# A two-layer convolutional decoder trunk on one core: other down blocks, no staging in the mixer, 34 weight units not staged

## The chip, the cores and the metric

The kernel runs on one core of one Trainium2 chip. The metric is device time in microseconds (us), the median of several runs, and lower is better. The engines are called as in the profile: PE (matmuls), DVE (vector), ACT (activations), POOL (GpSimd) and SP (here it only issues DMAs).

## What is computed

Two layers work on 1024 prompt tokens and on 8 sequences of 8 sample tokens, T = 1088 columns in all, with a width of 1024. Layer 0's token mixer is a gated short convolution, layer 1's a Conformer convolution module. All is float32.

```python
def short_conv_mixer(x, past, w_in, w_conv, w_out):
    bch = x @ w_in
    b, c, h = jnp.split(bch, 3, axis=-1)
    y, new_past = causal_dwconv(c * h, past, w_conv)
    return (b * y) @ w_out, new_past
def swiglu_ffn(x, w_gu, w_down):
    g, u = jnp.split(x @ w_gu, 2, axis=-1)
    return (jax.nn.silu(g) * u) @ w_down
...
        h = h + mix
        h = h + swiglu_ffn(rms_norm(h, g_ffn[i]), ffn_w_gu[i], ffn_w_down[i])
        gate = jax.nn.sigmoid(rms_norm(h, g_ple[i]) @ ple_w_gate[i])
        h = h + gate * (p[i] @ ple_w_proj[i])
```

The feed-forward has 2816 hidden features, 22 tiles of 128.

## The kernel before

**Products and weights.** Features lie on the 128 partitions and tokens along the columns, so `h` is eight tiles `h0` to `h7` of 128x1088. A float32 product is made of three products of a reduced type (fp32r): each operand is split into a high part (an ACT copy) and a low part (operand less its high part), and high·high, low·high and high·low are summed in PSUM. A weight *unit* is eight blocks of 128x128 (tile `wraw`, 128x1024). `prep_to` (lines 218 to 244) makes its high half on ACT (`whi`) and its low half (`wlo`) in one of two ways: by a POOL subtraction, or, where the unit has been *staged*, by a DMA from `dlo`.

**Staging.** `stage` (line 246) works ahead on the units of later parts, of which several are used more than once. One step handles half a unit: ACT's queue fetches `sraw`, ACT makes `shi`, POOL subtracts, and at the next step ACT's queue stores the result as `dlo`. The store waits for POOL, and whatever ACT has in its queue behind it waits too. A step is issued when a model clock of PE in the builder passes `stage_at`, every `STAGE_EVERY` us. `to_stage` (line 165) is the list of the halves.

**Mixer of layer 0.** `mixer_a` (line 525) calls `hidden` (line 649): `up(f)` computes one of eight activation tiles `act` (three items of eight blocks with the elementwise work on ACT, DVE and POOL), and a down block of n tiles adds, for each of eight outputs j, the sum over its n activation tiles to `h[j]`. `MIX_SPLIT` lists the block sizes. An item is one PSUM tile, of which there are two; `add_h` (line 517) is a DVE addition that frees it.

**End of the mixer.** In the last down block `mixer_end` (line 575) is called after each item. It adds, stores `h` for later, sums the squares for the next norm (`norm_stat`, tiles `sq` and `sqacc`), and makes the operands of the feed-forward (`op_first`, `op_sums`, `op_part`): high and low halves of B11, B21, B22 and of four sums T1 to T4 for each of four k, 28 operands of 128x544 twice. Where each lies is the table `cells`, filled in `last_down` (line 1215): memory of the mixer that has become free. `T4` and `B11` of the last k lend theirs to `sq` first.

**Feed-forward of layer 0, first half.** `ffn0_up` (line 669) computes gate and up of one hidden tile f by seven products in place of eight, each of 24 matmuls of 272 columns, on sums of operands and of weights (Strassen's scheme). The weight sums S1 to S4 (`ws`) of the next f are four DVE subtractions and additions in `pair_sums` (line 301); `pair_cell` (line 312) splits each of the seven weights A11 to S4 into a cell (`w`), those named A by POOL, those named S by DVE. The two raw tiles of a pair are fetched by `pair_fetch` when the cell A22 of the pair before is made. `next_weights(n)` (line 696) says behind which of the seven products which of these steps are issued: `m == 0` issues the sums, and 1 to 4 the cells. Engines carry out their instructions in the order in which they are issued.

**Second half.** `ffn0_down` (line 763) reads the stored hidden tiles back (`act_load`, tile `ta`), splits them (`act_split`: ACT `act`, DVE `act<-ta,act`) and multiplies in down blocks listed in `DOWN_0`, like the mixer's. `early` (line 1271) does this for the first block while the last hidden tile is computed, and loads `h` again in the order `DOWN_J`.

**Layer 1** prepares each unit some two ahead in the same `prep_to`; its feed-forward is run for the two halves of the tokens, so its units are fetched twice, and the last gate's units three times.

Line 129 is the helper through which every operation is issued, so all rows of the profile name it and are told apart by their tiles.

Of the kernel before, what the change touches and what calls it, by code (L numbers as in the profile page):

```python
# [145 lines left out]
class Net:  # L146
# [3 lines left out]
    def __init__(self, ctx, tc, xT, wall, pT, sa, sb, vecs, yT, sa_p, sa_s, sb_p, sb_s):  # L150
        self.ctx, self.tc, self.nc = ctx, tc, Engines(tc.nc)
        self.xT, self.wall, self.pT, self.sa, self.sb, self.vecs = xT, wall, pT, sa, sb, vecs
        self.yT, self.sa_p, self.sa_s, self.sb_p, self.sb_s = yT, sa_p, sa_s, sb_p, sb_s
        first = list(range(N_UNITS_0))
        middle = list(range(N_UNITS_0, N_UNITS_0 + N_PLE + N_PW1))
        proj = list(range(middle[-1] + 1, N_UNITS - N_UNITS_1))
        rest = list(range(N_UNITS - N_UNITS_1, N_UNITS))
        pw1 = middle[-N_PW1:]
        self.order = first + middle + middle[:-N_PW1] + proj[:1] + pw1 + proj[1:] + 2 * rest + rest[-KD:]
        self.raw, self.hi, self.lo = {}, {}, {}  # L160
        self.n_raw = self.n_prep = self.blk = 0
        self.limit = N_MIX
        self.n_conv = 0
        self.pairs, self.cell = {}, {}
        self.to_stage = deque((u, i) for u in dict.fromkeys(self.order[len(first):]) for i in range(2))
        self.staged, self.staging, self.stage_raw = {}, None, deque()
        self.stage_slots, self.stage_at, self.stage_ends = None, 0.0, False
        self.bg = deque()
        self.spare = []
        self.slots = deque(["w"] * self.RING)  # L170
        self.shift_late = True
        self.sums_split = True
        self.lanes = [deque(), deque()]
        self.lane_cost = [0.0, HALF_TILE]
        self.pe_later = []
# [349 lines left out]
    def mixer_a(self, y):  # L525
        nc = self.nc
        g = GJ
        r = self.rg(g)
        self.r2 = self.pu0.tile([P, T], F32, name="r2", bufs=1)
        acts = {}  # L530

        def up(f):
            u = self.pu0.tile([P, UA0_COLS], F32, name="u0", tag="u0")
            nc.gpsimd.memset(u[:, 0:LA], 0.0)
            nc.sync.dma_start(u[:, SMP_A:], self.sa[f])
            usm = smp(u[:, SMP_A:])
            t = self.tmp(g)
            if f == 0:
                psc, psh = self.pair(g, y)
                nc.scalar.activation(t, psc, AF.Copy)  # L540
            else:
                nc.scalar.activation(t, self.item(g, y), AF.Copy)
                self.stage_ends = f == KD - 1
                psh = self.item(g, y)
            nc.vector.tensor_tensor(u[:, LA:LA + SEQ], psh[:, :SEQ], t[:, :SEQ], ALU.mult)
            nc.vector.tensor_tensor(usm[:, :, LA:], smp(psh[:, SEQ:]), smp(t[:, SEQ:]), ALU.mult)
            if f == 0:
                psb = self.item(g, y, self.rms(g, 1, 4))
                b = self.tmp(g)
                nc.scalar.activation(b, psb, AF.Copy)  # L550
                psb = b
                nc.vector.tensor_tensor(self.r2, r, r, ALU.mult)
            for o, i in ((u[:, LA:LA + SEQ], self.r2[:, :SEQ]), (usm[:, :, LA:], smp(self.r2[:, SEQ:]))):
                nc.gpsimd.tensor_tensor(o, o, i, ALU.mult)
            nc.sync.dma_start(self.sa_p[f], u[:, SEQ:SEQ + LA])
            nc.sync.dma_start(smp(self.sa_s[f]), usm[:, :, LS:])
            w = self.vec("a_conv", f, CA)
            q = self.tmp(g)
            for k in reversed(range(CA)):
                for o, i in ((q[:, :SEQ], u[:, k:k + SEQ]), (smp(q[:, SEQ:]), usm[:, :, k:k + LS])):  # L560
# [12 lines left out]
        self.hidden(g, MIX_SPLIT, up, acts, js=MIX_J, last=self.mixer_end)

    def mixer_end(self, i, ps):
# [9 lines left out]
        self.hd[j] = self.pd.tile([P, T], F32, name=f"hd{j}")  # L585
        self.nc.sync.dma_start(self.hd[j], self.h[j])
        k = j - KH
        pool, tag = self.cells["B11", KH - 1] if i % 2 == 0 and i else self.cells["T4", KH - 2]
        stat = lambda: self.norm_stat(g, j, sq=i and pool.tile([P, T], F32, name="sq", tag=tag, bufs=1))
        if i == KD - 1:  # L590
            self.op_first(k)
            self.at_end[3](0)
# [76 lines left out]
    def ffn0_up(self, early):  # L669
# [11 lines left out]
        for f in range(KF):  # L681
# [14 lines left out]
            def next_weights(m):  # L696

                i = f + 1
                if i == KF:
                    return  # L700
                m -= 2 if f < 2 else 1
                if m == 0:
                    self.pair_sums(i)
                for n in {1: self.ORDER[:3], 2: self.ORDER[3:5], 3: self.ORDER[5:6], 4: self.ORDER[6:]}.get(m, ()):
                    self.pair_cell(i, n)
                if m == 4 and i + 1 < KF:
                    self.pair_fetch(i + 1)
# [39 lines left out]
            self.ad[f] = self.pd.tile([P, T], F32, name=f"ad{f}")  # L747
            nc.sync.dma_start(self.ad[f], t)

    def act_load(self, queue):  # L750
        f = len(self.acts)
        low, high = (pool.tile([P, T], F32R, name="act", tag=tag, bufs=1) for pool, tag in self.places.popleft())
        t = self.tmp(GJ, "ta")
        queue.dma_start(t, self.ad[f])
        self.acts.append((high, low))
        return t
# [6 lines left out]
    def ffn0_down(self, swap):  # L763
# [3 lines left out]
        for b, n in enumerate(DOWN_0):  # L767
            last = b == len(DOWN_0) - 1
            loads = []
            for i in range(KD):  # L770
# [3 lines left out]
                if b == len(DOWN_0) - 2 and j == KD - 3:  # L774
                    self.stage_ends = True
                self.add_h(g, j, self.item(g, self.acts[at:at + n]))
                if loads:
                    self.act_split(*loads.pop(0))
                if not last:
                    continue  # L780
# [373 lines left out]
    def run(self):  # L1154
# [35 lines left out]
        self.pps = pool("ps_j", c_ps, space=PSUM, bufs=2)  # L1190
        self.pY = pool("y_j", c_y, side="right", bufs=KD)
        self.pt = pool("t_j", c_t, bufs=4)
        self.pX = pool("x_j", c_x, bufs=4)
        self.pu0 = pool("u0", c_u, bufs=2)
        self.hd, self.ad, self.right, self.sums = {}, {}, {}, {}
        p = pool("stage_m", c_st)
        self.stage_with(self.stage_tiles(p, 0, 2), self.stage_tiles(p, 2, 6))
        self.stage_at = self.STAGE_FROM

        warm = self.pps.tile([P, 512], F32, name="st", tag="m0", bufs=1)[:, :P]  # L1200
        for _ in range(self.WARM):
# [11 lines left out]
            self.norm_stat(GJ, j, nc.vector)  # L1213

        def last_down():
            self.stage_with()
            c_st.close()
            c_u.close()
            c_y.close()
            py = pool("y_16", c_y, side="right")  # L1220
            py2 = pool("y_6", c_y2, side="right")
            self.cells = {}
            free = [(py, f"y{i}") for i in range(2 * KD)]
            for k in range(KH - 1):
                for n in ("B11", "T1"):
                    self.cells[n, k] = py2, f"z{len(self.cells)}"
            for k in range(KH - 1):
                for n in ("B21", "T2", "B22", "T3", "T4"):
                    self.cells[n, k] = free.pop(0)
            self.cells["B11", KH - 1] = free.pop(0)  # L1230
            for n, j in ("B21", 0), ("T1", 4), ("T2", 1), ("B22", 5), ("T3", 2), ("T4", 6):
                self.cells[n, KH - 1] = ph, f"h{j}"

        def before_last():
# [4 lines left out]
        def last_item():  # L1239
            c_x.close()  # L1240
            self.pws = pool("w2", c_x)
            self.ring = deque([(self.pw, f"w{i}") for i in (2, 5, 3, 6)] + [
                (self.pws, f"c{i}") for i in range(4)] + [(self.pw, f"w{i}") for i in (4, 7)])

# [17 lines left out]
        p = pool("stage_u", c_st)  # L1262
        self.stage_with(self.stage_tiles(p, 0, 1), self.stage_tiles(p, 1, 5))
        self.stage_at += self.STAGE_LATE
        py, py2 = self.cells["T2", 0][0], self.cells["B11", 0][0]
        places = [[(py2, f"z{2 * i}"), (py2, f"z{2 * i + 1}")] for i in range(3)]
        places += [[(py, f"y{2 * i}"), (py, f"y{2 * i + 1}")] for i in range(5)]
        self.places = deque(places[i % len(places)] for i in range(KF - DOWN_0[-1]))
        self.acts = []
# [1 line left out]
        def early():  # L1271
# [3 lines left out]
            self.limit = len(self.order)  # L1275
            self.n_conv += 2
            self.fetch_to(self.n_raw + self.RAW)
            t = [self.act_load(nc.sync) for _ in range(DOWN_0[0])]
            self.prep_to(self.n_raw - self.RAW + 1)
            for f in range(DOWN_0[0]):  # L1280
                self.act_split(f, t[f])
# [16 lines left out]
            lambda name, dtype, i=i: py.tile([P, T], dtype, name=name, tag=f"y{i}", bufs=1)[:, :WH]  # L1298
            for i in range(10, 16)]
        self.stage_with(at[:2], at[2:])  # L1300
        c_ya = ExitStack()

        def swap():
# [111 lines left out]
    RMS_AT = {GJ: (0, 2), GA: (3, 6), GB: (1, 4)}  # L1415
    T_BUFS = 5
    COST_B = 1.6
    STAGE_EVERY = 3.75
    STAGE_LATE = 25.0
    STAGE_FROM = 30.0  # L1420
    LAG = 3
    WARM = 12
    RB_GATE = 4
# [123 lines left out]
```

## Time and profile before

| | |
|---|---|
| time, median of 3 runs | 2551.46 us (2551.21 to 2556.66) |
| the profiled execution's own time | 2553.06 us |
| its span in the profile | 2551.3 us |
| mean granted clock of PE | 0.988 of full speed |
| PE busy | 2480.1 us, 97% |
| DVE busy | 1412.5 us, 55% |
| ACT busy | 1000.6 us, 39% |
| POOL busy | 969.9 us, 38% |
| moved by DMA | 462.71 MB, 181 GB/s |

The profile is of one execution; its own time lies 1.76 us above its span (launch and end) and 1.60 above the median of the runs. An engine's busy time is the sum of its instructions. In a row of a timeline stand the start, the duration, the engine, the line, the operation, the tile written and the tiles read, how many like it follow one another (x6) and, in brackets, the idle time of that engine just before and what ended it. In a row of windows, PEclk is the mean clock that PE was granted: 1.00 is 2.4 GHz, and the lower of its two levels is 1.2 GHz.

### The profile page before, as it was taken

How to read it: one execution, taken by the hardware profiler on the slowest of the kernel's cores; microseconds unless marked ns; L12 is line 12 of the kernel's file. 1: busy time of each engine (PE TensorE's matmuls, PEld its weight loads, DVE VectorE, ACT ScalarE, POOL GpSimd, SP SyncE). 2: the span in 40 equal slices, each digit the busy share in tenths (PEclk: the TensorE clock that was granted, in tenths of full speed). 3: DMA queues.
4: the chain of work that ended last, by engine and by line, in shares of the span. 5: the costliest groups of instructions: out<-in, count | busy, mean ns of one | idle time of the engine just before them, and what ended most of it. 6: DMA issues, size and time to landing. Idle time of an engine off the chain costs nothing.

```text
span 2551.3 us, 39084 instructions
## 1 busy us (share of the span) xinstructions
PE 2480.1 (97%) x15590; PEld 2286.9 (90%) x15590; DVE 1412.5 (55%) x1940; ACT 1000.6 (39%) x1377; POOL 969.9 (38%) x662
## 2 busy tenths in 40 slices
PE   9989998899999989999999999999999999999997
PEld 8888997899999989998789897888887999999997
DVE  6122128788888853324587676777874622222235
ACT  5322235344443433325555436444435532222235
POOL 3656554356665645533244233333341210000012
PEclk9999999999999999999999999999999999999999
DMA  4555542366665677643565566555556565555445
GB/s 145 166 166 164 162 129 87 111 204 207 207 210 199 214 266 235 223 149 109 177 211 180 172 176 190 190 183 190 189 175 206 202 246 200 162 164 164 165 165 194
DMA packets 183575, 462.71 MB, mean 181 GB/s; under 512 B 38368, under 2 KB 41824, under 8 KB 183392
## 3 DMA queue, kind: packets, MB, share of 16 engines
q1 hardware_dynamic: 116000, 331.46, 39.5%
q10 hardware_dynamic: 67392, 128.74, 15.9%
q8 instruction: 123, 2.02, 0.3%
q14 instruction: 60, 0.49, 0.1%
HBM read 375.65 MB, written 84.48 MB: 180 GB/s over the span
## 4 chain that ended last, share of the span: by engine, by line
PE 60%; DVE 3%; DMA 2%; ACT 1%; issue 1%; POOL 1%; ACTq 0%; DVEq 0%; POOLq 0%; SPq 0%
PE ps L129 60%; DMA ta<-ad 1%; DVE t L129 1%; POOL sraw L129 1%; DVE ws L129 0%; DMA wlo<-dlo 0%; DVE h L129 0%; DVE acc L129 0%; ACT ua L129 0%; DVE hna L129 0%; DVE nt L129 0%; ACT shi L129 0%; ACT cact L129 0%; DMA wraw<-wall 0%; ACT act L129 0%
## 5 line engine op out<-in xcount | busy, mean ns | idle before, releaser
L129 PE MATMUL ps<-hn,whi 128*128 128x288 f32 (+3 forms) x4416 | 916.5, 324 | 5.7 <-ACT t L129 3.4
L129 PEld LDWEIGHTS ps<-hn,whi 128*128 128x128 f32 x4416 | 693.9, 189 | 61.2 <-ACT t L129 3.7
L129 PE MATMUL ps<-hn,wlo 128*128 128x288 f32 (+3 forms) x2208 | 563.3, 323 | 3.0 <-DMA wlo<-dlo 3.0
L129 PE MATMUL ps<-act,whi 128*128 128x288 f32 (+1 forms) x2496 | 520.1, 333 | 23.6 <-DVE h L129 19.5
L129 PE MATMUL ps<-y,w 128*128 128x272 f32 x3696 | 475.0, 291 | 18.1 <-ACT t L129 6.2
L129 PEld LDWEIGHTS ps<-y,w 128*128 128x128 f32 x3696 | 472.9, 191 | 20.0 <-ACT t L129 6.5
L129 PEld LDWEIGHTS ps<-act,whi 128*128 128x128 f32 x2496 | 393.4, 191 | 64.8 <-DVE h L129 19.1
L129 POOL TENSOR_TENSOR sraw<-sraw,shi 128x512 fp32r<-128x512 f32 x220 | 320.1, 1455 | 203.8 <-ACT shi L129 90.4
L129 PEld LDWEIGHTS ps<-hn,wlo 128*128 128x128 f32 x2208 | 365.5, 189 | 29.9 <-DMA wlo<-dlo 3.2
L129 ACT ACTIVATE whi<-wraw 128x1024 fp32r<-128x1024 f32 (+1 forms) x282 | 293.4, 1042 | 186.7 <-PE ps L129 144.7
L129 DVE TENSOR_TENSOR h<-ps,h 128x1088 f32<-128x1088 f32 (+2 forms) x200 | 184.9, 927 | 245.6 <-PE ps L129 245.3
L129 PE MATMUL ps<-act,wlo 128*128 128x288 f32 (+1 forms) x1248 | 306.0, 331 | 0.0
L129 POOL TENSOR_TENSOR t<-t,r 128x512 f32<-128x512 f32 (+2 forms) x52 | 80.4, 1547 | 538.1 <-ACT t L129 493.0
L129 ACT ACTIVATE shi<-sraw 128x512 fp32r<-128x512 f32 x220 | 138.0, 627 | 359.8 <-POOL sraw L129 355.9
L129 POOL TENSOR_TENSOR sqacc<-sqacc,sq 128x512 f32<-128x512 f32 (+4 forms) x76 | 115.7, 1522 | 314.4 <-ACT sq L129 314.1
L129 DVE TENSOR_TENSOR t<-ps,t 128x544 f32<-128x544 f32 (+3 forms) x155 | 113.6, 743 | 217.6 <-PE ps L129 170.7
L129 PEld LDWEIGHTS ps<-act,wlo 128*128 128x128 f32 x1248 | 201.2, 191 | 18.8
L129 ACT ACTIVATE t<-t 128x512 f32<-128x512 f32 (+4 forms) x106 | 76.0, 718 | 302.1 <-DVE t L129 302.0
L129 POOL TENSOR_TENSOR prod<-prod 128x512 f32<-128x512 f32 x96 | 124.3, 1304 | 182.5 <-ACT prod L129 182.3
L129 POOL TENSOR_TENSOR wlo<-wraw,whi 128x1024 fp32r<-128x1024 f32 (+1 forms) x54 | 134.8, 2499 | 145.3 <-ACT whi L129 141.8
L129 DVE TENSOR_TENSOR t<-ps,r 128x512 f32<-128x512 f32 (+3 forms) x116 | 79.0, 684 | 189.4 <-PE ps L129 188.6
L129 POOL TENSOR_TENSOR w<-wraw,w 128x512 fp32r<-128x512 f32 x66 | 102.0, 1547 | 103.1 <-ACT w L129 103.0
(154 smaller groups left out, 2465.3 us busy)
## 6 DMA issues: line engine op xcount, KB each, us to landing
wraw<-wall SPq DMA_DIRECT2D x322, 512.0 KB, 3.7
wlo<-dlo SPq DMA_DIRECT2D x226, 512.0 KB, 3.7
sraw<-wall ACTq DMA_DIRECT2D x220, 256.0 KB, 3.4
dlo<-sraw ACTq DMA_DIRECT2D x220, 256.0 KB, 3.0
ad<-t SPq DMA_DIRECT2D x22, 544.0 KB, 4.6
ta<-ad ACTq DMA_DIRECT2D x20, 544.0 KB, 5.6
h<-xT SPq DMA_DIRECT2D x8, 544.0 KB, 6.2
hd<-h SPq DMA_DIRECT2D x8, 544.0 KB, 2.7
```

The costliest lines, as they stand in the source:

```text
L129: return f(out, *args, **kw)
```

## The change

1. The mixer's down blocks have 3 and 5 tiles, where there were blocks of 2, 2 and 4. `act` gets five buffers for four.
2. The mixer stages nothing; its staging tiles are gone, and `STAGE_FROM` with them.
3. Of layer 1's last units 34 are no longer staged: 26 in the feed-forward, used twice each, and 8 of the gate, used three times. Staging has 152 halves for 220. `STAGE_EVERY` goes from 3.75 to 3.6. `STAGE_LATE` goes from 25 to 10, and ffn0_down's staging starts `2*STAGE_LATE` late.
4. The last down block adds its squares on DVE in place of POOL. The `cells` are laid out anew, and `sq` lies in cells of B22 and T1.
5. In ffn0_up the weight steps come one product later from the third unit on too (`m -= 2` always).
6. The first down block of ffn0_down has three tiles and the last three; the third `ta` lies in `h7`'s place, `h` is loaded in another order, and the splits of later blocks begin at their third item.

```diff
-MIX_SPLIT = [2, 2, 4]
+MIX_SPLIT = [3, 5]
-DOWN_J = [3, 7, 1, 2, 4, 5, 0, 6]
-DOWN_0 = [2, 4, 4, 4, 4, 4]
+DOWN_J = [3, 0, 1, 5, 2, 6, 4, 7]
+DOWN_0 = [3, 4, 4, 4, 4, 3]
...
-        self.to_stage = deque((u, i) for u in dict.fromkeys(self.order[len(first):]) for i in range(2))
+        kept = [u for i, u in enumerate(rest[:-KD]) if i < KD or i % 5 not in (2, 4)]
+        self.to_stage = deque((u, i) for u in middle + proj + kept for i in range(2))
...
-        pool, tag = self.cells["B11", KH - 1] if i % 2 == 0 and i else self.cells["T4", KH - 2]
-        stat = lambda: self.norm_stat(g, j, sq=i and pool.tile([P, T], F32, name="sq", tag=tag, bufs=1))
+        pool, tag = self.cells["B22" if i % 2 == 0 else "T1", KH - 2]
+        stat = lambda: self.norm_stat(
+            g, j, self.nc.vector, sq=i and pool.tile([P, T], F32, name="sq", tag=tag, bufs=1))
...
-                m -= 2 if f < 2 else 1
+                m -= 2
...
-                if loads:
+                if i > 1 and loads:
                     self.act_split(*loads.pop(0))
...
-        self.pX = pool("x_j", c_x, bufs=4)
+        self.pX = pool("x_j", c_x, bufs=5)
...
-        p = pool("stage_m", c_st)
-        self.stage_with(self.stage_tiles(p, 0, 2), self.stage_tiles(p, 2, 6))
-        self.stage_at = self.STAGE_FROM
...
-            t = [self.act_load(nc.sync) for _ in range(DOWN_0[0])]
+            t = [self.act_load(nc.sync, i == 2 and ph.tile([P, T], F32, name="ta", tag="h7"))
+                 for i in range(DOWN_0[0])]
...
+        self.stage_at += 2 * self.STAGE_LATE
...
-    STAGE_EVERY = 3.75
-    STAGE_LATE = 25.0
-    STAGE_FROM = 30.0
+    STAGE_EVERY = 3.6
+    STAGE_LATE = 10.0
```

In the mixer, on ACT, a part of the second up tile before (`t` and `u` are its convolution, `act` its result, `shi`, `sraw` and `dlo` staging):

```order
L129 ACTIVATE shi<-sraw 128x512
L129 DMA sraw<-wall 128x512
L129 DMA dlo_757<-sraw 128x512
L129 ACTIVATE shi<-sraw 128x512
L129 DMA sraw<-wall 128x512
L129 ACTIVATE act<-t 128x1088
L129 ACTIVATE whi<-wraw 128x1024
L129 DMA dlo_830<-sraw 128x512
```

and the same engine and tile in the change:

```order
L129 ACTIVATE t<-ps 128x1088
L129 ACTIVATE whi<-wraw 128x1024
L129 ACTIVATE t<-u_477,vecs_sb 128x1024
L129 ACTIVATE t<-u_477,vecs_sb 128x64
L129 ACTIVATE whi<-wraw 128x1024
L129 ACTIVATE act<-t 128x1088
L129 ACTIVATE whi<-wraw 128x1024
```

Two stores and two `shi` that stood ahead of `act<-t` are gone from ACT's queue.

In ffn0_up, on ACT, one hidden unit before (`w<-ws` is the cell of a sum, `w<-wraw` of A12 and A22, `t<-t` the silu):

```order
L129 ACTIVATE w_8594<-ws 128x512
L129 ACTIVATE w_8597<-ws 128x512
L129 DMA dlo_8544<-sraw 128x512
L129 ACTIVATE shi<-sraw 128x512
L129 DMA sraw<-wall 128x512
L129 ACTIVATE w_8632<-wraw 128x512
L129 DMA dlo_8648<-sraw 128x512
L129 ACTIVATE shi<-sraw 128x512
L129 DMA sraw<-wall 128x512
L129 ACTIVATE t<-t 128x1088
L129 ACTIVATE w_8670<-wraw 128x512
```

and in the change:

```order
L129 ACTIVATE w_8203<-ws 128x512
L129 ACTIVATE w_8206<-ws 128x512
L129 DMA dlo_8216<-sraw 128x512
L129 ACTIVATE shi<-sraw 128x512
L129 DMA sraw<-wall 128x512
L129 ACTIVATE t<-t 128x1088
L129 ACTIVATE w_8244<-wraw 128x512
L129 DMA dlo_8216<-sraw 128x512
L129 ACTIVATE shi<-sraw 128x512
L129 DMA sraw<-wall 128x512
L129 ACTIVATE w_8280<-wraw 128x512
```

The cell of A12 has moved behind the silu, and in 15 of some 20 units a staging step stands between it and A22's.


## Rows read from the trace of the kernel before

**Rows 1.** Windows: start:end, length, busy of PE, PEld, DVE, ACT, POOL, PEclk, DMA.

```profile
106.00:145.00 39.00, 27.70 (x134) 24.32 (x133) 9.72 (x11) 12.39 (x17) 23.34 (x15) 0.82 0.57 166
236.00:247.00 11.00, 6.60 (x27) 5.66 (x26) 3.92 (x4) 4.13 (x6) 6.31 (x4) 0.69 0.67 223
411.00:460.00 49.00, 31.96 (x172) 29.32 (x171) 40.84 (x46) 23.74 (x34) 15.83 (x7) 0.83 0.22 78
508.00:513.00 5.00, 4.65 (x25) 4.65 (x26) 5.00 (x7) 3.04 (x6) 4.02 (x3) 0.66 0.57 190
915.00:945.00 30.00, 22.55 (x112) 19.25 (x111) 16.64 (x16) 9.45 (x10) 9.64 (x4) 0.89 0.81 309
1551.00:1900.00 349.00, 348.77 (x1499) 282.20 (x1499) 263.16 (x568) 147.44 (x203) 123.11 (x96) 1.00 0.57 189
```

**Rows 2.** Timeline of PE in the mixer, from 121 to 141 us: start, duration, instruction, wait.

```profile
123.25 1.16 PE L129 MATMUL ps<-act,whi 128*128 128x288 f32 x6
...
139.11 2.18 PE L129 MATMUL ps<-act,whi 128*128 128x288 f32 x6 [4.94 <-DVE h L129]
```

**Rows 3.** Timeline of ACT in the mixer, from 128 to 137 us.

```profile
132.02 0.63 ACT L129 ACTIVATE shi<-sraw 128x512 fp32r<-128x512 f32 x1 [7.79 <-POOL sraw L129]
...
135.42 1.11 ACT L129 ACTIVATE act<-t 128x1088 fp32r<-128x1088 f32 x1 [0.26 <-issue]
```

**Rows 4.** Timeline of PE, end of the mixer and start of the feed-forward.

```profile
413.97 2.18 PE L129 MATMUL ps<-act,whi 128*128 128x288 f32 x6 [2.70 <-DVE h L129]
...
427.01 5.70 PE L129 MATMUL ps<-y,w 128*128 128x272 f32 x30 [3.08 <-DVE h L129]
...
452.42 5.67 PE L129 MATMUL ps<-y,w 128*128 128x272 f32 x24 [6.23 <-ACT t L129]
...
508.35 3.94 PE L129 MATMUL ps<-y,w 128*128 128x272 f32 x18 [3.71 <-DVE s L129]
```

**Rows 5.** Timelines of ACT, POOL and DVE between 425 and 437 us.

```profile
428.58 0.75 ACT L129 ACTIVATE y<-h,vecs_sb 128x544 fp32r<-128x544 f32 x1 [2.68 <-POOL sqacc L129]
...
435.08 3.06 POOL L129 TENSOR_TENSOR sqacc<-sqacc,sq 128x1088 f32<-128x1088 f32 x1 [6.53 <-ACT sq L129]
...
429.37 0.79 DVE L129 SCALAR_TENSOR_TENSOR y<-h,vecs_sb,y 128x544 fp32r<-128x544 f32 x1 [2.50 <-ACT y L129]
431.10 0.79 DVE L129 SCALAR_TENSOR_TENSOR y<-h,vecs_sb,y 128x544 fp32r<-128x544 f32 x1 [0.95 <-ACT y L129]
...
435.82 2.92 DVE L129 TENSOR_TENSOR ya<-yb,ya 128x544 f32<-128x544 f32 x1
```

**Rows 6.** Timelines of DVE, ACT and POOL, one unit of ffn0_up, cells issued late.

```profile
482.10 0.69 DVE L129 TENSOR_TENSOR ws<-wraw 128x512 f32<-128x512 f32 x1 [4.78 <-DMA wraw<-wall]
...
492.01 1.29 DVE L129 TENSOR_TENSOR t<-t,r 128x1088 f32<-128x1088 f32 x1
...
504.46 1.15 DVE L129 TENSOR_TENSOR ws<-wraw 128x512 f32<-128x512 f32 x1 [6.19 <-DMA wraw<-wall]
...
493.34 1.12 ACT L129 ACTIVATE t<-t 128x1088 f32<-128x1088 f32 x1 [4.37 <-DVE t L129]
...
496.45 2.34 POOL L129 TENSOR_TENSOR sraw<-sraw,shi 128x512 fp32r<-128x512 f32 x1
498.75 1.29 POOL L129 TENSOR_TENSOR w<-wraw,w 128x512 fp32r<-128x512 f32 x1
```

**Rows 7.** Timelines of DVE and PE in ffn0_up, 840 to 915 us, cells issued early.

```profile
861.43 0.69 DVE L129 TENSOR_TENSOR ws<-wraw 128x512 f32<-128x512 f32 x1 [1.08 <-DMA wraw<-wall]
...
881.88 1.40 DVE L129 TENSOR_TENSOR ws<-wraw 128x512 f32<-128x512 f32 x1 [2.10 <-DMA wraw<-wall]
...
839.48 75.72 PE L129 MATMUL ps<-y,w 128*128 128x272 f32 x600
```

**Rows 8.** Timeline of PE, start of ffn0_down.

```profile
915.62 1.24 PE L129 MATMUL ps<-act,whi 128*128 128x288 f32 x6 [0.41 <-DVE t L129]
```

**Rows 9.** Timeline of POOL in the mixer, one subtraction of a whole weight unit.

```profile
88.52 2.40 POOL L129 TENSOR_TENSOR wlo<-wraw,whi 128x1024 fp32r<-128x1024 f32 x1
```

More of the change, by code (lines that the diff above doesn't have):

```diff
@@ L542, in up @@
                 nc.scalar.activation(t, self.item(g, y), AF.Copy)
-                self.stage_ends = f == KD - 1
                 psh = self.item(g, y)
@@ L748, in ffn0_up, with act_load @@
             nc.sync.dma_start(self.ad[f], t)
-    def act_load(self, queue):
+    def act_load(self, queue, t=None):
         f = len(self.acts)
         low, high = (pool.tile([P, T], F32R, name="act", tag=tag, bufs=1) for pool, tag in self.places.popleft())
-        t = self.tmp(GJ, "ta")
+        t = t or self.tmp(GJ, "ta")
         queue.dma_start(t, self.ad[f])
@@ L1215, in last_down @@
         def last_down():
-            self.stage_with()
-            c_st.close()
             c_u.close()
@@ L1220, in last_down @@
             py = pool("y_16", c_y, side="right")
[L1221 to L1231, printed above, removed]
+            py2 = pool("y_4", c_y2, side="right")
+            free = [(py2, f"z{i}") for i in range(4)] + [(py, f"y{i}") for i in range(2 * KD)]
+            self.cells = {(n, k): free.pop(0) for n in ("B11", "T2", "T3", "T1", "B22", "B21") for k in range(KH - 1)}
+            self.cells.update({("T4", k): free.pop(0) for k in range(KH - 2)})
+            for n, j in ("B11", 0), ("B21", 4), ("T2", 1), ("T3", 5), ("T1", 2), ("B22", 6):
                 self.cells[n, KH - 1] = ph, f"h{j}"
@@ L1241, in last_item @@
             self.pws = pool("w2", c_x)
+            for k in (KH - 2, KH - 1):
+                self.cells["T4", k] = self.pws, f"y{k}"
             self.ring = deque([(self.pw, f"w{i}") for i in (2, 5, 3, 6)] + [
@@ L1264, in run @@
         self.stage_at += self.STAGE_LATE
-        py, py2 = self.cells["T2", 0][0], self.cells["B11", 0][0]
-        places = [[(py2, f"z{2 * i}"), (py2, f"z{2 * i + 1}")] for i in range(3)]
+        py, py2 = self.cells["T3", 0][0], self.cells["B11", 0][0]
+        places = [[(py2, f"z{2 * i}"), (py2, f"z{2 * i + 1}")] for i in range(2)]
         places += [[(py, f"y{2 * i}"), (py, f"y{2 * i + 1}")] for i in range(5)]
```

## The prediction

> **What bounds the kernel now.** I read the busy shares first: PE is busy for 97% of the span, so the whole kernel is one row of matmuls and only PE's gaps and its clock can give time back or take it. Then I listed PE's gaps with what released each, and took the windows in which they lie. The reader sees in [rows 1] five places that matter here. In the mixer PE stands for 39 − 27.70 = 11.30 us between 106 and 145 us and 11 − 6.60 = 4.40 us between 236 and 247, 15.70 in all; at the end of the mixer it stands 17.04 of 49; behind that 3.71 once [rows 4]; in the first block of ffn0_down 7.45 of 30. The granted clock in these windows is 0.82, 0.69, 0.83, 0.66 and 0.89, elsewhere 1.00: PE fell from 2.4 to 1.2 GHz behind the long gaps, and six matmuls that take 1.16 us take 2.18 [rows 2]. In the last 76 us of ffn0_up PE has no gap at all: 600 matmuls in 75.72 us make 21.20 us for a unit's 168 [rows 7].
>
> **A, the mixer.** Which engine is late there? ACT. A staging step waits on ACT's queue for POOL's subtraction, up to 7.79 us, and the split `act<-t` that PE needs next stands behind it [rows 3]. All staging in the mixer goes, and with it these waits. A down item of two blocks takes PE 3.0 us (one block of nine matmuls 1.5 [rows 2]); items of three and five take 4.5 and 7.5, so DVE's additions (1.29 for 1088 columns [rows 6]) fall behind less. I let all 15.70 go. The half clock: the mean of 0.82 over 39 us between the levels 1.0 and 0.5 makes 14.0 us at half speed, that of 0.69 over 11 makes 6.8; 20.8 together, with PE busy for some three quarters of it and half of that lost: 8.0. A = −23.7. Bounds: 0 if DVE's additions, not ACT, are what is late (the waits name `h`), and −26.1 with PE busy through all the slow stretch.
>
> **B, the end of the mixer.** An item of five blocks covers 7.5 us of the other engines' work, one of four 6.0. The waits for `h` of 2.70 and 3.08 [rows 4] go: −5.8. Then comes a chain that PE cannot cover: from the last addition through the sums to `t<-ps`, with PE waiting 6.23 at its end. In it ACT waits 2.68 for POOL's square sums, since the new cell's memory still holds squares, and DVE waits 2.50 and 0.95 for ACT [rows 5]; DVE's `ya<-yb,ya` takes 2.92 where a 544-column operation takes 0.79, while POOL adds its squares for 3.06 beside it [rows 5]. The new cells and the addition on DVE take these off (−2.50 − 0.95 − 2.13) and put one addition of 1.29 onto DVE [rows 6]: −4.3. With one slow stretch of three fewer (0.83 over 49 us is 16.7 us at half, at 32/49 busy 5.4 lost) −1.8. B = −11.9; bounds −5 (only the chain) to −17 (all gaps).
>
> The Trainium skill says the same of the 2.92 ("SBUF — State Buffer", "Who interferes with whom": a VectorE instruction with two SBUF inputs and a GpSimd instruction that reads SBUF exclude each other, whichever issues first). By this rule, the trace agrees, the move of the sum from POOL to DVE helps here; it has a side that speaks against the change, below.
>
> **C, ffn0_up.** Here the change gives time away. The DVE sums of the next pair of weight units are issued a product later in 20 units, and the cell A12 behind the silu. Now one circle closes: sums, silu of the unit, the cells A12 and A22 on ACT and POOL, which set the raw weights free, the fetch of the next pair, sums. The kernel before runs its first two units in this order, and so shows the circle once: sums start at 482.10, silu at 493.34, POOL is done with A22 at 500.04 (498.75 + 1.29), the next sums start at 504.46 after 6.19 of waiting for the fetch [rows 6]. That is 22.36 us where PE needs 21.20. It is what made PE wait 3.71 at 508.35 [rows 4]. In the early order sums came 20.45 apart and PE never waited [rows 7]. So from the third unit on PE will follow the circle.
>
> How long is it in the steady state? Two corrections. The sums ran there at 0.69 each, 2.8 for four; beside POOL they start with 1.15 or 1.40 [rows 6, 7], up to 5.0 for four: +2.2. And a staging step, 2.34 on POOL and 0.63 with its wait on ACT [rows 6, 3], 3.6 with handing over, stood in the measured circle; in a quarter of the new units one is missing: −0.9. That gives 22.4 to 23.7, and I take the middle, 23.0. From S1's start at 452.42 the loop is then 29.7 to the sums of 482.10, 0.8 for staging that begins 15 us earlier, 19 circles, and a tail of 27.8 (eleven products of 24 matmuls, 3.02 each, are 33.2, of which PE has run 5.4 ahead in four PSUM buffers): 58.3 + 19 × 23.0 = 495.3. Before it was 915.21 − 452.42 = 462.8 (915.62 less its wait of 0.41 [rows 8]). C = +32.5; bounds: with 22.36 it is +20.6, with 23.65 +44.9. I put no fall of the clock into it: PE then waits some 1.8 us per unit, and the gaps with a fall in their window here are of 2.70 us and longer [rows 2, 4].
>
> **D, the start of ffn0_down.** 7.45 of gaps and, at 0.89 over 30 us, 6.6 us at half, so 3.3 lost. Three acts at hand and an item of 4.5 us cover more, but the third `act` comes about 2 us later, split included, and DVE ends the loop with its own lag. I take 4.8 of gaps and 1.7 of half clock: −4.3; bounds −10.8 to 0.
>
> **E, units not staged.** 34 units, 26 used twice and 8 three times: 76 subtractions of 2.40 us [rows 9] on POOL, 182 us, in place of as many transfers. In layer 1's feed-forward POOL is busy 123 of 349 us [rows 1]; 26 more make 185 of 349. The units are prepared two ahead, so these lie beside PE: +1.5 for a late one here and there, bounds 0 to +10. STAGE_LATE and STAGE_EVERY shift staging within C; their price is in it.
>
> **Sum.** −23.7 − 11.9 + 32.5 − 4.3 + 1.5 = −5.9. The profiled execution took 2553.06, 1.60 above the median of the runs: 2547.2 there, 2545.6 on the median.
>
> **Rivals.**
> 1. *The circle hides in PE.* The measured circle had a fetch wait of 6.19, two staging steps and a loop that had only begun; if freed DVE time brings it to 21.2 or less, C is not +32.5 but −5.4 (the 3.71 and its half clock go), and D goes to about −7, as the loop ends without lag. −23.7 − 11.9 − 5.4 − 7 + 1.5 = −46.5: 2505. For it: in the early order PE never waited [rows 7]; against: the one measured circle of the late order is 22.36.
> 2. *The circle is longer: slower.* Same place, all its staging steps hit, and DVE's weight sums and subtractions are doubled by POOL: the early order's circle of 20.45, with A12 and A22 both behind the silu and one staging step between (+3.6), is 24.0 or more. 58.3 + 19 × 24.0 = 514.3, C = +51.5, sum +13.1: 2564.6. The change breaks even at a circle of 23.3 and is slower by over 0.2% from 23.6. For it: the DMA wait of 6.19; against: 8 of 20 units had a lighter mix.
> 3. *POOL's subtractions hold DVE in layer 1.* `ya<-yb,ya` shows DVE held for 2.1 us by one POOL operation [rows 5]. The 76 new ones read SBUF as well; if each second holds a DVE subtraction that PE waits for, 26 × 2.40 = 62 a pass at most, some +25 all told: 2571. The rule of the Trainium skill above, by whichever issues first, makes such waits possible; no row of layer 1 shows one. Against: PE is busy 348.77 of 349 us there, beside the 123 us that POOL works there already [rows 1].
> 4. *The mixer's waits stay.* A five-block item also makes the acts come later; DVE remains behind, A is near 0 with C as forecast: 2569.
>
> **How the numbers follow.** A measurement of this kernel tells about 0.2%, 5.1 us, from no change: faster is below 2546.4, slower above 2556.6. The forecast (circle between 22.4 and 23.6, 2532 to 2557) has 0.48, of which 0.30 fall faster and 0.18 within; rival 1 has 0.21, all faster; rival 2 0.20, rival 3 0.05, rival 4 0.06, of which 0.01 is within and the rest slower. So 0.51, 0.19, 0.30. The likeliest case's own range is 2532 to 2557. For 8 in 10 it must reach to rival 1, 2503, and to the near half of rival 2, 2566.
>
> **What would show it.** The spacing of `ws` in ffn0_up: 22.4 to 23.6 if right, 21.2 for rival 1. PE's waits there: about 1.8 each unit for DVE. In the mixer no wait above 1 us and a clock of 1.00 from 20 to 411 us. A wait of about 2 us before `t<-ps` at the transition. `wlo<-wraw,whi` 76 times more on POOL, and PE still busy throughout layer 1. I am wrong if the mixer's gaps return under another releaser, or if the loop's spacing leaves 22.4 to 23.6.

## The result and the profile after

The change made the kernel slower: 2575.77 us median of 4 runs (2574.88 to 2578.14) against 2551.34 (2547.74 to 2556.66), a ratio of 1.0095 with an interval of 1.0076 to 1.0115. I had forecast 2545.6 with a range up to 2566. The profiled execution took 2575.43 with a span of 2573.6, 22.3 more than before. The same matmuls, found by their order in both traces, show where they lie (S1 is the product with the sum S1; pw2 is the second pointwise product of layer 1's convolution module):

| stretch | before | after | difference | forecast |
|---|---|---|---|---|
| start to S1 of the first hidden unit | 452.42 | 417.25 | -35.2 | A + B: -35.6 |
| S1 to the end of ffn0_up | 462.8 | 501.0 | +38.2 | C: +32.5 |
| ffn0_down and layer 0's gate | 493.1 | 489.0 | -4.1 | D: -4.3 |
| to the last down block of the first half of the tokens in layer 1 | 540.4 | 542.2 | +1.8 | E: +1.5 for this and all below |
| that block, the gate, the second half's pw2 | 122.6 | 129.05 | +6.4 | |
| the second half's feed-forward up to its last down item | 395.5 | 395.6 | +0.1 | |
| that block, two gates, the final norm, to the end of the span | 84.4 | 99.5 | +15.1 | |

Up to layer 1 the forecast's steps are right to 6 us, and the change is worth nothing there: -35.2 + 38.2 - 4.1. The loss is made behind it, in the stretches with a gate. Windows view of the changed kernel (columns as in [rows 1]):

```profile
20.00:395.00 375.00, 373.92 (x2266) 341.39 (x2264) 124.61 (x131) 96.31 (x108) 115.89 (x64) 1.00 0.18 56
394.00:420.00 26.00, 14.71 (x90) 14.09 (x91) 23.45 (x31) 14.60 (x22) 3.31 (x1) 0.80 0.23 83
471.00:892.00 421.00, 396.98 (x3042) 392.54 (x3042) 308.67 (x343) 157.54 (x261) 234.12 (x154) 0.98 0.59 194
514.00:520.00 6.00, 5.68 (x33) 5.68 (x34) 2.62 (x4) 1.53 (x3) 3.54 (x3) 0.72 0.95 292
915.00:945.00 30.00, 23.76 (x139) 21.75 (x138) 15.67 (x14) 10.40 (x10) 10.48 (x4) 0.89 0.93 369
1949.50:2078.50 129.00, 125.60 (x724) 111.43 (x724) 73.67 (x80) 63.69 (x84) 55.50 (x31) 0.99 0.50 176
2474.10:2561.60 87.50, 75.23 (x521) 73.17 (x521) 67.91 (x81) 47.17 (x77) 60.74 (x35) 0.93 0.23 77
```

In the mixer PE is busy for 373.92 of 375 us at a clock of 1.00, where [rows 1] had 11.30 and 4.40 us of gaps at 0.82 and 0.69. The loop of ffn0_up (471 to 892) leaves 24 us idle at a clock of 0.98; the row from 514 to 520 lies in it. The last two rows are the stretches with a gate. The same two stretches of the kernel before:

```profile
1948.80:2071.40 122.60, 122.60 (x724) 110.67 (x725) 59.60 (x80) 63.58 (x84) 29.54 (x21) 1.00 0.65 225
2466.90:2539.30 72.40, 69.66 (x521) 69.21 (x521) 44.21 (x81) 47.90 (x77) 21.08 (x20) 1.00 0.56 195
```

The matmuls are the same 724 and 521. DVE's busy time goes from 59.60 to 73.67 and from 44.21 to 67.91 us, though its work there did not change; POOL's goes from 29.54 to 55.50 and from 21.08 to 60.74, by subtractions of weights. In all there are 130 of them, 76 more than before (the page's group of this name):

```profile
L129 POOL TENSOR_TENSOR wlo<-wraw,whi 128x1024 fp32r<-128x1024 f32 (+1 forms) x130 | 319.3, 2458 | 458.6 <-ACT whi L129 439.2
```

Timeline of PE after, seven places where it waits:

```profile
396.40 1.93 PE L129 MATMUL ps<-y,w 128*128 128x272 f32 x7 [2.40 <-DVE h L129]
...
417.25 3.09 PE L129 MATMUL ps<-y,w 128*128 128x272 f32 x12 [8.30 <-ACT t L129]
...
514.32 2.03 PE L129 MATMUL ps<-y,w 128*128 128x272 f32 x12 [1.90 <-ACT t L129]
...
924.47 1.91 PE L129 MATMUL ps<-act,whi 128*128 128x288 f32 x5 [6.24 <-DVE t L129]
...
2009.15 0.50 PE L129 MATMUL ps<-hn,wlo 128*128 128x512 f32 x1 [1.78 <-POOL wlo L129]
...
2536.79 0.64 PE L129 MATMUL ps<-sh,ones_r 128*128 128x320 f32 x1 [4.51 <-ACT sh L129]
...
2561.58 1.22 PE L129 MATMUL ps<-sqacc,ones 128*128 128x256 f32 x2 [5.20 <-POOL sqacc L129]
```

2.40 is left of [rows 4]'s 2.70 and 3.08. S1 starts 20.85 us behind the matmul with this wait, where it was 25.41, though the wait before S1 is now 8.30 for 6.23. 1.90 is one of the loop's waits. The last three are new or larger, all in the stretches with a gate: PE waits for `wlo` itself, for `sh` (the split of the summed squares, which is late) and for `sqacc`, 5.20 where it was 2.69. The window of 87.5 us has a clock of 0.93, before it was 1.00: the clock fell twice in it, from 2498 to 2502 us (0.60) behind four waits of 0.92 and less for `hn`, and again behind the wait for `sh`. Behind the wait for `sqacc` it is low up to the end, as it was before the change.

Timeline of DVE, and below it of POOL, in the last gate of the changed kernel: an operand of its matmuls, one item, and the first and the last row of its two last items of 320 columns:

```profile
2481.36 2.71 DVE L129 SCALAR_TENSOR_TENSOR hn<-h,vecs_sb,hn 128x576 fp32r<-128x576 f32 x1 [0.85 <-ACT hn L129]
...
2515.14 0.48 DVE L129 TENSOR_TENSOR t<-ps,r 128x320 f32<-128x320 f32 x1
2515.54 2.29 DVE L129 TENSOR_TENSOR t<-t,ub 128x320 f32<-128x320 f32 x1
2517.87 1.05 DVE L129 TENSOR_TENSOR h<-h,t 128x320 f32<-128x320 f32 x1
2518.84 0.48 DVE L129 TENSOR_TENSOR t<-ps,r 128x320 f32<-128x320 f32 x1
...
2526.25 0.48 DVE L129 TENSOR_TENSOR t<-ps,r 128x320 f32<-128x320 f32 x1
...
2532.65 1.03 DVE L129 TENSOR_TENSOR h<-h,t 128x320 f32<-128x320 f32 x1
...
2514.82 2.66 POOL L129 TENSOR_TENSOR wlo<-wraw,whi 128x1024 fp32r<-128x1024 f32 x1
2517.45 1.12 POOL L129 TENSOR_TENSOR sqacc<-sqacc,sq 128x320 f32<-128x320 f32 x1
```

and of DVE in the same places before (an item, then the two last):

```profile
2506.47 0.49 DVE L129 TENSOR_TENSOR t<-ps,r 128x320 f32<-128x320 f32 x1 [2.10 <-PE ps L129]
2506.88 0.48 DVE L129 TENSOR_TENSOR t<-t,ub 128x320 f32<-128x320 f32 x1
2507.39 0.49 DVE L129 TENSOR_TENSOR h<-h,t 128x320 f32<-128x320 f32 x1
2509.99 0.49 DVE L129 TENSOR_TENSOR t<-ps,r 128x320 f32<-128x320 f32 x1 [2.10 <-PE ps L129]
...
2513.51 0.49 DVE L129 TENSOR_TENSOR t<-ps,r 128x320 f32<-128x320 f32 x1 [2.10 <-PE ps L129]
...
2515.36 0.49 DVE L129 TENSOR_TENSOR h<-h,t 128x320 f32<-128x320 f32 x1
```

Before, `t<-t,ub` and `h<-h,t` take 0.48 and 0.49, and DVE then waits 2.10 us for PE, which needs 3.52 per item. Now `t<-t,ub` takes 2.29 and ends just behind POOL's `wlo` (2514.82 + 2.66 = 2517.48), and `h<-h,t` takes 1.05 beside POOL's square sum. The two are 2.37 longer, which is more than the 2.10 that DVE had to spare: items start 3.70 apart on DVE.

DVE thus falls some 0.2 us further behind PE with each item, but that alone does not hold PE. The same matmuls of the two traces tell where the 15.1 us of the last stretch are lost. PE comes 4.4 us behind at the start of the gate: `hn`, its operand, took 2.71 and 2.76 on DVE beside two subtractions, 0.82 before. Through the eight items it stays at 4.4. Then 4.7 go at the wait for `sh`: behind the eight items PE has 7.3 us of other matmuls and then needs `sh`, which needs the last `h`. From the last `t<-ps` of the items to the last `h` DVE takes 7.43 us (2526.25 to 2533.68), where it took 2.34 (2513.51 to 2515.85). 3.4 more go behind this wait, at a low clock, and 2.6 at the end. In the first gate, of the 6.4 us, 1.7 go at `hn` in the same way and 4.0 at and behind the wait for `wlo`: ACT made that unit's `whi` behind a square that had waited 3.34 for a held `h`, and a unit that is not staged needs POOL's 2.43 on top.

### The profile page after: what moved, and what is told of

Same layout as the page of the kernel before. It is cut to its first block, busy times and chain, and to the rows that moved or that the text cites. A ratio compares the mean times of both kernels' runs of the same rounds, so it can differ in the third digit from the quotient of the medians.

```text
span 2573.6 us, 38622 instructions
## 1 busy us (share of the span) xinstructions
PE 2489.4 (97%) x15590; PEld 2290.8 (89%) x15590; DVE 1425.2 (55%) x1939; ACT 959.0 (37%) x1309; POOL 1049.2 (41%) x663
## 4 chain that ended last, share of the span: by engine, by line
PE 54%; DVE 6%; ACT 2%; issue 1%; DMA 1%; POOL 0%; SPq 0%; DVEq 0%; ACTq 0%; POOLq 0%
PE ps L129 54%; DVE t L129 2%; DVE h L129 1%; DVE hn L129 1%; DMA wraw<-wall 0%; DVE nt L129 0%; ACT whi L129 0%; ACT hn L129 0%; DMA ta<-ad 0%; POOL wlo L129 0%; DVE acc L129 0%; DMA wlo<-dlo 0%; DVE ub L129 0%; DVE nv L129 0%; DVE hna L129 0%
## 5 line engine op out<-in xcount | busy, mean ns | idle before, releaser
L129 PE MATMUL ps<-y,w 128*128 128x272 f32 x3696 | 486.4, 294 | 39.1 <-DVE s L129 13.9
L129 PEld LDWEIGHTS ps<-y,w 128*128 128x128 f32 x3696 | 479.6, 193 | 45.7 <-ACT t L129 14.8
L129 PE MATMUL ps<-act,whi 128*128 128x288 f32 (+1 forms) x2496 | 512.6, 329 | 6.9 <-DVE t L129 6.2
L129 POOL TENSOR_TENSOR wlo<-wraw,whi 128x1024 fp32r<-128x1024 f32 (+1 forms) x130 | 319.3, 2458 | 458.6 <-ACT whi L129 439.2
L129 DVE TENSOR_TENSOR h<-ps,h 128x1088 f32<-128x1088 f32 (+2 forms) x192 | 174.5, 911 | 220.5 <-PE ps L129 220.3
L129 POOL TENSOR_TENSOR sraw<-sraw,shi 128x512 fp32r<-128x512 f32 x152 | 228.6, 1504 | 114.3 <-ACT shi L129 74.0
L129 ACT ACTIVATE shi<-sraw 128x512 fp32r<-128x512 f32 x152 | 95.2, 626 | 225.5 <-POOL sraw L129 195.9
L129 POOL TENSOR_TENSOR sqacc<-sqacc,sq 128x512 f32<-128x512 f32 (+4 forms) x69 | 101.1, 1465 | 188.3 <-ACT sq L129 185.0
```

The costliest lines, as they stand in the source:

```text
L129: return f(out, *args, **kw)
```

## The experiments

Eleven kernels ran, in three sets with the kernel before beside each set (its medians there: 2555.53, 2554.60, 2552.92). So ratios to it are compared, not times. All differences are edits to the changed kernel unless it is said otherwise.

**gate_staged**, the place of the unstaged units:

```diff
-        kept = [... if i < KD or i % 5 not in (2, 4)]
+        kept = [... if i < KD or i % 2] + rest[-KD:]
```

> The changed kernel with the gate's 8 units staged again, and 33 of the 66 other units of layer 1's feed-forward unstaged (26 before), so that staging has 154 halves (152). Theory 1 (the units of the gate, used three times where DVE and POOL both have work for PE, are the cost): of the 24 us the changed kernel loses, the windows of the gates hold 6.4 (1949 to 2078 us) and 15.2 (2474 us to the end); both go, 14 more subtractions in the feed-forward cost nothing: 2575.8 - 21.6 = 2554. Theory 2 (it is the number of subtractions on POOL, wherever they are): 14 more for 24 fewer, about 40% of the price goes at most: 2566 or more. Theory 3 (the end is late for a reason of its own, such as the phase of the clock): no change, 2576.

Ratio 1.0015 (1.0004 to 1.0026), 2558.82 us: 0.80% of the 0.95% is gone, though 33 units of the feed-forward are unstaged for 26. The stretches with a gate take 122.57 and 84.2 us, as before the change. Theory 1. In the feed-forward's first pass, though, 4.5 us are added:

```profile
1911.74 2.40 POOL L129 TENSOR_TENSOR wlo<-wraw,whi 128x1024 fp32r<-128x1024 f32 x1 [7.46 <-ACT whi L129]
...
1915.34 1.74 DVE L129 TENSOR_TENSOR ub<-ub,rs 128x576 f32<-128x576 f32 x1 [4.76 <-POOL ub L129]
...
1919.42 0.73 PE L129 MATMUL ps<-act,whi 128*128 128x512 f32 x2 [3.55 <-DVE h L129]
```

The wait of PE lies in the last but one down block of the pass. An unstaged unit's subtraction stands ahead of `ub` on POOL, DVE waits 4.76 for that with an addition to `h` behind it, and PE 3.55. So the subtractions are not free in the feed-forward either, wherever POOL has a step that DVE waits for.

**early_sums**, the loop:

```diff
-                m -= 2
+                m -= 2 if f < 2 else 1
```

> The changed kernel with the weight sums of ffn0_up one product earlier from the third unit on, as before the change. Theory 1 (the circle of sums, silu, cells and fetch of 23.2 us costs what stands above PE's 21.2): the loop from S1's start takes 457 to 460 in place of 501, and the down part behind it starts with 2 us less: 2575.8 - 42 = 2533. Theory 2 (staging every 3.6 us from the start of the loop is what makes the circle long, in either order): the sums come 22.5 us apart, the loop takes 487: 2561.

0.9921 (0.9905 to 0.9937), 2537.31 us: -1.74% against the change, some 44 us. PE has no idle time left in the loop, with the staging of the change in it:

```profile
494.00:880.00 386.00, 385.59 (x3062) 385.24 (x3061) 333.43 (x344) 160.55 (x261) 236.22 (x152) 1.00 0.64 213
```

Theory 1; the rival, that staging makes the circle long in either order, falls. The late sums also cost time behind the loop: ffn0_down and the gate take 483.6 us here, 489.0 in the change.

**both**, the two edits together.

> The two edits together: gate staged, sums early. If both theories 1 hold and do not touch each other: 2575.8 - 21.6 - 42 = 2512, which is 39 below the kernel before. If the loop's PE time is then bound by something else (staging, fetches): 2525 to 2540.

0.9861 (0.9845 to 0.9878), 2520.83 us. The gains add up: 0.80 + 1.74 = 2.54% expected from the two ratios, 2.34% measured.

**mix_224**, the mixer's blocks:

```diff
-MIX_SPLIT = [3, 5]
+MIX_SPLIT = [2, 2, 4]
```

> The changed kernel with the mixer's blocks at 2, 2 and 4 again, still without staging in the mixer. Theory 1 (staging's waits on ACT made the mixer's gaps): no gap of over 1 us up to 390 us; only the end of the mixer loses, by its 4-tile items: +5 us, 2581. Theory 2 (the blocks of two tiles made them, since DVE's work for an activation and its eight additions does not fit beside them): the four gaps of 15.7 us in all come back with their half clock: +24 and more, 2600.

1.0106 (1.0090 to 1.0121), 2583.27 us. Its PE timeline from the last items of the mixer on; there is no gap of over 1 us between 9 us and the first of these rows:

```profile
392.90 1.51 PE L129 MATMUL ps<-act,whi 128*128 128x288 f32 x4 [3.63 <-DVE h L129]
...
406.77 1.50 PE L129 MATMUL ps<-y,w 128*128 128x272 f32 x10 [2.91 <-DVE h L129]
...
427.61 1.73 PE L129 MATMUL ps<-y,w 128*128 128x272 f32 x6 [8.29 <-ACT t L129]
```

Theory 1: staging made the mixer's gaps. The matmul that waits for the last `h` starts at 406.77 here, at 427.01 before and at 396.40 in the change: leaving out staging gave 20.2 us (with what the new cells and square sums do up to there), the blocks of 3 and 5 gave 10.4, by items that cover more of DVE's work at the mixer's end alone. That is in the traces; the ratios of this kernel and the change, 1.0106 and 1.0095, differ by less than their intervals. From this matmul to S1 it is 20.85 us in this kernel as in the change, 25.41 before: the cells and the square sums gave the remaining 4.6.

That the gaps came from ACT's queue, and not from staging's POOL work holding DVE, is read from the trace of before, at the longest of the gaps. DVE stood 7.23 us for ACT's `act`, which came behind the staging steps of [rows 3], and the two additions behind it took 1.24 each, no longer than elsewhere:

```profile
136.56 1.29 DVE L129 TENSOR_TENSOR act<-t,act 128x1088 fp32r<-128x1088 f32 x1 [7.23 <-ACT act L129]
```

**gate_squares_dve**, lock or queue:

```diff
-                self.norm_stat(g, j)
+                self.norm_stat(g, j, nc.vector)
```

> The changed kernel with the square sums of the gates (in ple1) added on DVE in place of POOL. It tells apart how the gate's unstaged units cost. Theory lock (POOL's subtraction holds DVE's two-input instructions, which go from 0.49 to 2.30 us, and DVE is late): DVE is held as before and has eight additions more per pass: no gain, 2576 to 2584. Theory queue (the squares stand behind the subtractions on POOL, and the norm waits for the squares): the waits of 4.51 for sh and 5.20 for sqacc go with their half clock: 2564 to 2568.

1.0118 (1.0102 to 1.0135), 2584.82 us: no gain, as the lock has it. A square sum on DVE is held like the others, and PE waits 8.18 for `sh` where it waited 4.51:

```profile
2515.03 2.09 DVE L129 TENSOR_TENSOR sqacc<-sqacc,sq 128x320 f32<-128x320 f32 x1 [0.88 <-ACT sq L129]
...
2517.44 2.29 DVE L129 TENSOR_TENSOR t<-t,ub 128x320 f32<-128x320 f32 x1
...
2543.39 0.63 PE L129 MATMUL ps<-sh,ones_r 128*128 128x320 f32 x1 [8.18 <-ACT sh L129]
```

**gate_pool_writes**, POOL as busy, without reading SBUF. Edit to gate_staged:

```diff
+                if self.order[u] >= N_UNITS - KD:
+                    for _ in range(8):
+                        nc.gpsimd.memset(self.scratch, 0.0)
```

> The kernel gate_staged with, for each of the gate's units, eight POOL memsets of 128x256 (an estimate of 2.5 us, by 122 ns for 30 columns and 98 for 2) into a tile that nobody reads: POOL is as busy as with the subtraction, but reads no SBUF. Theory lock: DVE is not held, t<-t,ub takes 0.49, and the gates take as long as in gate_staged, within 3 us; so the total is that of gate_staged. Theory queue: squares and half clock are as late as in the changed kernel: 15 to 21 us more than gate_staged.

1.0028 (1.0018 to 1.0037), 2561.67 us, 0.13% (3 us) above gate_staged. The gates at the end, one item of DVE, and POOL beside it:

```profile
2472.00:2547.00 75.00, 70.26 (x519) 68.97 (x517) 43.87 (x78) 48.86 (x79) 56.67 (x132) 1.00 0.50 176
...
2511.99 0.49 DVE L129 TENSOR_TENSOR t<-ps,r 128x320 f32<-128x320 f32 x1 [2.10 <-PE ps L129]
2512.40 0.48 DVE L129 TENSOR_TENSOR t<-t,ub 128x320 f32<-128x320 f32 x1
2512.91 0.49 DVE L129 TENSOR_TENSOR h<-h,t 128x320 f32<-128x320 f32 x1
...
2510.56 2.89 POOL L129 MEMSET scratch<- 128x256 f32 x8
```

POOL is busy for 56.67 us, nearly as long as with the subtractions, and the eight memsets take 2.90; DVE's busy time is 43.87, as before the change, `t<-t,ub` takes 0.48, and DVE waits 2.10 for PE again. Of the 21.5 us some 3.5 are POOL's queue (from the last down item to the last square sum 75.2 us, 72.4 in gate_staged, 87.5 in the change, and 0.7 in the first gate); most of the rest is DVE being held. Two differences stay: memsets wait for nothing, where a subtraction waits for ACT's `whi`, and no matmul waits for a memset, so the 4.0 us at `wlo` in the first gate are not tested by this kernel.

**stat_pool**, the square sums of the mixer's end:

```diff
-            g, j, self.nc.vector, sq=i and ...
+            g, j, sq=i and ...
```

> The changed kernel with the square sums of the mixer's end on POOL again. By the prediction's step B the move to DVE took 2.13 off (ya<-yb,ya held for 2.92) and put 1.29 on, and the rest of the chain's gain came from the cells: the stretch from the first product to S1 (20.85 us now, 25.4 before) grows by 1 to 3 us. If the whole gain of 4.6 came from this move: +4.6. If DVE's extra addition weighs more than the hold: 0 to -1.3.

1.0089 (1.0074 to 1.0104), 2577.19 us. From the matmul that waits for the last `h` in the change to S1 it is 24.00 us for 20.85, and `ya` is held again beside POOL:

```profile
403.75 2.92 DVE L129 TENSOR_TENSOR ya<-yb,ya 128x544 f32<-128x544 f32 x1
...
403.02 3.06 POOL L129 TENSOR_TENSOR sqacc<-sqacc,sq 128x1088 f32<-128x1088 f32 x1 [4.48 <-ACT sq L129]
```

So 3.2 of the chain's 4.6 came from this move, slightly over what was expected. But the move has a price just ahead of the chain: here PE does not wait for the last `h` at all, where it waits 2.40 in the change. From the first matmul of the feed-forward to S1, with this wait in it, it is 26.27 us here, 25.66 in the change and 24.65 in both, spread and down_2, whose mixers are the change's. Net, the move gave 0.6 to 1.6 us. In the kernel's time it is not seen: the spans are 2573.7 and 2573.6.

**spread**, edit to both: unstaged units only among the feed-forward's first 58.

```diff
+        kept = [... if i < KD or i >= 66 or i % 7 in (1, 3, 5)] + rest[-KD:]
```

> The kernel both, with the 33 unstaged units of the feed-forward taken from its first 58 units alone, none from the last 8. In gate_staged and both PE waits 3.5 us in the last down block of the first pass, where an unstaged unit's subtraction stands on POOL ahead of ub, for which DVE waits 4.76. If that is the cause: the wait and its half clock go, -5 us against both. If more units lying closer together fall behind in the earlier blocks: 0 or slower than both.

0.9854 (0.9839 to 0.9869), 2517.61 us, the fastest of all: 1.5% below the kernel before. The step from both, 0.07%, is within the intervals, so the 5 us are not shown. PE's wait, in the last but one down block, goes from 3.49 to 1.35 and the first pass from 414.2 to 411.45 us; but the stretches around this pass grow by as much, and from layer 0's gate to the second half's pw2 both traces have 668.7 us.

**before_late**, edit to the kernel before:

```diff
-                m -= 2 if f < 2 else 1
+                m -= 2
```

> The kernel before with one edit of the change alone: the weight sums one product later in every unit. Theory (the circle alone is the price of step C, whatever the mixer, the cells and the staging list): sums 23 to 24 us apart, the loop from S1's start 36 to 44 us longer than 462.8, and the down block's start a little later: before + 40 = 2592. If the circle needs the new cells or the denser staging to be long: before + 0 to 25.

1.0130 (1.0109 to 1.0151), 2587.35 us: +33. The first and the last of 19 sums of weights in steady state:

```profile
505.83 0.69 DVE L129 TENSOR_TENSOR ws<-wraw 128x512 f32<-128x512 f32 x1 [5.34 <-DMA wraw<-wall]
...
919.10 1.58 DVE L129 TENSOR_TENSOR ws<-wraw 128x512 f32<-128x512 f32 x1 [6.22 <-DMA wraw<-wall]
```

18 circles (from one start of the sums to the next) in 413.27 us are 22.96 each. The loop took 492.7 us from S1, 29.9 more than before. The loop is below what I expected, and the whole is above the 25 us that the rival allowed: the circle alone makes most of the price. The change's own loop is 8 us longer, through 0.27 us in each of the 18 circles and 3.2 in the one before them; whether its earlier and denser staging does that was not separated.

**down_2**, the first down block:

```diff
-DOWN_0 = [3, 4, 4, 4, 4, 3]
+DOWN_0 = [2, 4, 4, 4, 4, 4]
```

> The changed kernel with ffn0_down's blocks at 2, 4, 4, 4, 4, 4 again, all else as changed. By step D the first block of three is worth 4.3 us: 2575.8 + 4 = 2580, with PE's waits of 3.2 and 2.8 for h back behind the block's first items. If the order in which h is loaded and the later splits made that gain: no change, 2576.

1.0083 (1.0063 to 1.0103), 2574.74 us: no change. Its down block's start (window from the loop's end on):

```profile
919.90:944.00 24.10, 19.45 (x109) 17.43 (x108) 15.99 (x16) 7.90 (x8) 6.40 (x3) 0.93 0.98 367
```

4.65 us idle at 0.93; the change has 6.24 idle there and 0.89 over its 30 us. From the loop's end to the layer's gate it is 489.8 us, 489.0 in the change. So by these traces the block of three gives no more than 0.8 of step D's 4.1 us. What else the change does here, the new order of loading `h`, the later splits, and staging that begins later and is sparser, was not tried piece by piece.

**spread_26**, edit to spread: 26 unstaged units, a step every 3.3 us.

> The kernel spread with 26 unstaged units in place of 33 and a staging step every 3.3 us in place of 3.6. If the remaining price of unstaged units in the feed-forward (2.6 us in the first pass) is by their number: -1 us against spread. If a denser staging lengthens the early circle beyond PE's 21.2: +5 to +20.

0.9877 (0.9857 to 0.9897), 2522.79 us: no gain. The first pass takes 410.8 for 411.45, and the loop 470 us from S1 for 462: a denser staging costs the loop more than 14 fewer subtractions (seven units, used twice) give.

## Why the prediction was wrong

**The step that failed is E**: "The units are prepared two ahead, so these lie beside PE: +1.5", with bounds of 0 to +10. It cost 23.4 us: 1.8 in the first feed-forward, 0.1 in the second, and 6.4 and 15.1 where a gate is. I looked for what waits for `wlo`, found PE's cover long enough, and checked POOL's busy share in the feed-forward. What waits is DVE, for POOL's subtraction to end. I had the mechanism as rival 3 at a chance of 0.05, with 2571 as its time, but laid it in the feed-forward, where a DVE instruction that is held is mostly covered (26 subtractions a pass for these 1.8 and 0.1). That its 2571 comes within 5 us of the measured time is luck. In a gate PE needs 3.52 us per item, DVE had 2.10 to spare in each, and six of the eight items of the last gate meet a subtraction of 2.4 to 2.7. So DVE's slack is gone, and PE pays where its own work runs out while it needs DVE's result: at `hn` ahead of the items, and behind them, where it stood for `sh` and its clock fell.

The spare time could be read from the rows of the gates, at the end of the trace of before; I had written of the 8 gate units and then argued with 26. Rival 3 says that no row of layer 1 shows a DVE instruction held. One does, in that gate, beside a square sum:

```profile
2500.53 1.10 DVE L129 TENSOR_TENSOR h<-h,t 128x320 f32<-128x320 f32 x1
...
2500.40 0.88 POOL L129 TENSOR_TENSOR sqacc<-sqacc,sq 128x320 f32<-128x320 f32 x1 [12.16 <-ACT sq L129]
```

The Trainium skill ("SBUF — State Buffer", "Who interferes with whom") states that a VectorE instruction with two SBUF inputs contends with a GpSimd instruction that reads SBUF, and not with one that only writes it. The runs agree on both halves: 2.29 us beside a subtraction, 0.48 beside memsets.

**C was right in kind and short in size.** The circle was forecast at 23.0 us:

```profile
447.61 0.69 DVE L129 TENSOR_TENSOR ws<-wraw 128x512 f32<-128x512 f32 x1 [4.11 <-DMA wraw<-wall]
...
473.11 1.40 DVE L129 TENSOR_TENSOR ws<-wraw 128x512 f32<-128x512 f32 x1 [3.52 <-DMA wraw<-wall]
...
891.33 1.53 DVE L129 TENSOR_TENSOR ws<-wraw 128x512 f32<-128x512 f32 x1 [3.29 <-DMA wraw<-wall]
```

From 473.11 on, 418.22 us for 18 of them are 23.23. The forecast's sum has 19, from the sums of 447.61, and the first of these is 25.50: 443.7 us in all, 23.35 each, where 437.0 was forecast. The way to these sums took 30.4 us (30.5 forecast) and the tail 26.9 (27.8), which gives the measured 501.0. I had put no fall of the clock in it; it fell behind several waits, among them the one of 1.90 (0.72 from 514 to 520 us). Whether these falls lengthen the circle was not separated. The lower bound of +20.6 should read +20.3 by its own terms. early_sums and before_late show the step in both directions. The price of the late sums does not end with the loop: ffn0_down behind it takes 5.4 us longer in the change than in early_sums.

**A and B** summed to -35.6 and measured -35.2, divided otherwise: staging took 20.2 where I had 23.7 for the mixer, the longer items 10.4 where I had 7.6, the chain 4.6 where I had 4.3. That the sum is right to 0.4 us is partly luck. mix_224 and the trace of before bear out that staging on ACT's queue, not DVE's additions, made the mixer wait. In B the waits for `h` did not all go: 2.40 is left, and stat_pool shows that it comes with the squares on DVE, which I had priced in the chain alone. The wait before S1, for which I expected about 2 us, is 8.30.

**D** measured -4.1 for -4.3, which is luck: its terms of 4.8 and 1.7, less the 2 for the third `act`, make 4.5, down_2 shows that the block of three gives 0.8 at most, and with the sums early the same stretch is worth 9.5 (483.6 for 493.1).

**Rivals.** 1 (the circle hides) fell: 23.23. 2 (a circle of 24) fell. 3 (POOL holds DVE) came true, in the gates. 4 (the mixer's waits stay) fell. With E at its forecast the sum of the measured steps would have been +0.4, no change; C's 5.7 beyond its forecast would have taken the gain, E made the loss.

## What to carry to other kernels

Moving work to an idle engine has a price at every engine that it can hold up: before a POOL operation that reads memory is put beside DVE, compare its length with DVE's idle time per item in each stage where it lands, the shortest stage first, and look at the places where PE's own work runs out and it needs DVE's result. A unit that is used three times in short items is the worst candidate, and a rarely waited-for one in long items the best: choosing 33 other units and taking back the line on the weight sums turned 1% of loss into 1.4 to 1.5% of gain (both, spread). A loop of several engines that closes through a buffer is a bound of its own; measure its circle once in the trace and multiply.

## What had not been expected of the hardware

In these rows it is the instruction that starts second that lengthens, whichever engine it is on. The subtraction at 2481.05 us took 2.41 and held DVE's `hn` for 2.71; the one at 2514.82 started while `h<-h,t` (2514.17, 1.04 us) was under way and took 2.66, as did four more in the last gate that started so (2.64 to 2.67). `h<-ps,h`, with one operand in PSUM, took its usual 0.76 beside the subtraction at 2474.32.

The falls of the clock in the trace before stood behind waits of PE of 2.69 us and more. In the change it also fell behind waits of 1.90 (0.72 from 514 to 520) and 1.78 (at 2009.15), and at 2498 behind four of 0.92 and less close together, but not behind one of 2.41 (at 827.42).
